# Attention keys of two branches stored tile by tile in pairs, with one mask product per score tile

## The chip, the cores and the metric

The kernel runs on one core of one Trainium2 chip. The metric is device time in microseconds (us) of one execution; lower is better. Beside the time of a run there is the span of a profiled execution, from its first to its last recorded instruction.

## What is computed

One layer of a hybrid block on 512 tokens of width 1024, in fp32: a normalised input projection, an mLSTM branch with 4 heads, a sparse attention branch (NSA) with 8 heads in 2 key groups, an output projection, a gated feed-forward net with a short convolution, a gated extra embedding and a last normalisation. Only the attention scores bear on the change. For each head and query the reference forms three softmaxes: over up to 31 compressed keys, over the selected keys and over a window of keys.

```python
s_c = einsum(qblk, Kc) - slope * dist_c
p_c = where(valid_c, softmax(where(valid_c, s_c, NEG)), 0.0)
s_s = where(valid_s, einsum(qblk, Ksel) - slope * dist_s, NEG)
p_s = softmax(s_s)
s_w = einsum(qblk, kwin) - slope * dist_w
p_w = softmax(where(valid_w, s_w, NEG))
out = gate_c * (p_c @ Vc) + gate_s * (p_s @ Vsel) + gate_w * (p_w @ vwin)
```

With 512 tokens there are 8 selectable blocks and 16 may be selected, so all are; and the window is 512 wide. Both branches are therefore full causal attention over 512 keys, with different keys and values. Below, s is the selected branch, w the window branch, c the compressed one.

## The kernel before, in words

Every fp32 matrix is split into a high and a low part of type float32r and multiplied as three products, so TensorE does several passes for each projection. ScalarE makes the high part (L166), VectorE the low part (L167).

**Order of work.** A `Stream` (L182) holds the projections as jobs that yield matmul by matmul. The attention code is written out by hand, and between its pieces it calls `st.fill(us)`, which emits so many microseconds (by the planner's own costs) of the next projections: filler for TensorE. `FILL2` (L49) is the filler after each of the first four score tiles, `FILL0` and `FILL1` (L47, L48) that of the later ones. When the jobs run out, `fill` emits nothing. `PE_ORDER` is False, so the compiler's list scheduler may still move instructions of an engine past each other, and the order on TensorE is fixed at compile time.

**Keys.** `K` (L464) has 32 columns of compressed keys, then 512 of s, then 512 of w, as high and low part and with rows for position and causal mask of the compressed keys. `key_evac` (L483) writes a branch's columns after its projection: four ScalarE copies (L491) and two VectorE differences (L492) a branch, 512 elements each. The positions come by DMA from `kpos` (L726; made on the host at L1413).

**Scores.** `scores(g, i, r)` (L754) makes one score tile: 128 queries (tile i of 4) of one head (4g + r) against 32 + 2n key columns, n = 128(i + 1). There are 32 such tiles, in the order of `groups` (L861): g = 0 with i = 3, 2, 1, 0, then g = 1 with i = 0, 1, 2, 3. A tile takes these steps:

- products with the high part of the keys (L786) and with the low part (L788), in column regions that each lie in one PSUM bank of 512 columns: one region of 320 columns for i = 0 (two strided pieces of 160), 288 and 256 for i = 1, 416 and 384 for i = 2, and 272, 272 and 512 for i = 3;
- the causal mask of the diagonal 128 columns, added by a bf16 product of an identity with a mask tile (L790): one of 256 columns for i = 0, where s and w are neighbours, and two of 128 columns for the other i;
- row maxima on VectorE: c (L791), s and w together (L793) for i < 3, or s (L795) and w (L796) apart for i = 3;
- three exponentials on ScalarE with row sums (L803), in the order c, s, w;
- the reciprocal (L805), and the scaling of the three parts on GpSimd, for r = 3 partly on VectorE (L810).

**PSUM.** All eight banks belong to one pool: `Sa` (two banks, one buffer), `Sb` (one bank, one buffer), `G`, `T` (two buffers of one bank each) and `V`. Score tiles with i < 3 lie in `Sa`. Those with i = 3 are two tiles, `s_3a` in `Sa` (c and s) and `s_3b` in `Sb` (w), which are released separately. The mLSTM stage uses the same two buffers for `pb` (L999) and `ms` (L1017), the input stage for `pmv` and `pc`.

**Values.** For each group, `value_turn` (L822) transposes four heads' tiles (L835), ScalarE and VectorE split the result (L838, L839), and `value_product` (L842) multiplies it with the values (L843, L845). The scores of the next group are emitted between these units. The last group, g = 1 with i = 3, has no next group; only filler lies between its units.

Of the kernel before, what the change touches and what calls it, by code (L numbers as in the profile page):

```python
# [7 lines left out]
F32 = mybir.dt.float32  # L8
# [3 lines left out]
AF = mybir.ActivationFunctionType  # L12
ALU = mybir.AluOpType
AX = mybir.AxisListType

S = 512
# [29 lines left out]
LOADS = 3  # L46
FILL0 = 0.35  # L47
FILL1 = (2.0, 1.35, 0.9, 0.65)  # L48
FILL2 = 2.5  # L49
MF0 = 1.4  # L50
MF1 = 0.7
MF2 = 1.4
# [16 lines left out]
def f32(ap):  # L69
    return ap.bitcast(F32)  # L70
# [3 lines left out]
def hybrid_block_kernel(ctx: ExitStack, tc: tile.TileContext, a, out):  # L74
    nc = tc.nc
    TE, VE, SE, GE = nc.tensor, nc.vector, nc.scalar, nc.gpsimd
# [5 lines left out]
    tmp = ctx.enter_context(tc.tile_pool(name="tmp", bufs=4))  # L82
    psum = ctx.enter_context(tc.tile_pool(name="psum", bufs=1, space=bass.MemoryType.PSUM))

    def bank(tag, bufs, n, name):
        shape = [128, 512] if n == 1 else [128, n, 512]
        return psum.tile(shape, F32, tag=tag, bufs=bufs, name=name)

    def pSa(name):
        return bank("Sa", 1, 2, name)  # L90

    def pSb(name):
        return bank("Sb", 1, 1, name)

    def pG(name):
        return bank("G", 2, 1, name)

    def pT(name):
        return bank("T", 2, 1, name)
# [6 lines left out]
    def pW(name):  # L106
        wide[0] += 1
        return pG(name) if wide[0] % 2 else pT(name)

    def t2k(name, dt=F32):  # L110
        return tmp.tile([128, 512], dt, tag="t2k", name=name)
# [150 lines left out]
    identb = consts.tile([128, 128], BF, name="identb")  # L262
    maskt = consts.tile([128, 128], BF, name="maskt")
# [199 lines left out]
    NK = 32 + 2 * S  # L463
    K = apool.tile([128, 2, 2, NK], F32R, tag="K", name="K")  # L464
# [18 lines left out]
    def key_evac(br):  # L483
        def evac(ps):
            z = t2k(f"zk{br}")
            VE.tensor_mul(z, ps, rb1)
            sl = slice(32 + br * S, 32 + (br + 1) * S)
            for g in range(2):
                zg = z[g * 64:(g + 1) * 64]
                for half in (g, 1 - g):  # L490
                    SE.activation(K[half * 64:(half + 1) * 64, g, 0, sl], zg, AF.Copy)  # L491
                VE.tensor_sub(K[0:64, g, 1, sl], zg, f32(K[g * 64:(g + 1) * 64, g, 0, sl]))  # L492
        return evac

    cx = {}
# [252 lines left out]
    st.until("mv3")  # L748
    mixa = main.tile([128, 2, 4, S], F32R, tag="mixa", name="mixa")
    mv_done()  # L750

    Ec = {}

    def scores(g, i, r):  # L754
        h = 4 * g + r
        n = (i + 1) * 128
        lq = slice(i * 128, (i + 1) * 128)
        kh, kl = K[:, g, 0], K[0:98, g, 1]
        qa, qb = Q[g][:, 0, r, lq], Q[g][0:98, 1, r, lq]
        nm = tmp.tile([128, 3], F32, tag="nm", name=f"nm{h}_{i}")  # L760
        if i == 0:
            ps = pSa(f"s{h}_{i}")
            v = lambda t: t.rearrange("p (b n) -> p b n", n=512)[:, :, 0:160]
            reg = [(ps[:, 0, 0:320], v(kh[:, 0:1024]), v(kl[:, 0:1024]))]
            cm, sm, wm = ps[:, 0, 0:32], ps[:, 0, 32:160], ps[:, 0, 192:320]
            sw = ps[:, 0, 32:352].rearrange("p (b n) -> p b n", b=2)[:, :, 0:128]
        elif i < 3:
            ps = pSa(f"s{h}_{i}")
            reg = [(ps[:, 0, 0:32 + n], kh[:, 0:32 + n], kl[:, 0:32 + n]),
                   (ps[:, 1, 32:32 + n], kh[:, 32 + S:32 + S + n], kl[:, 32 + S:32 + S + n])]  # L770
            cm, sm, wm = ps[:, 0, 0:32], ps[:, 0, 32:32 + n], ps[:, 1, 32:32 + n]
            sw = ps[:, :, 32:32 + n]
        else:
            p1, p2 = pSa(f"s{h}_{i}a"), pSb(f"s{h}_{i}b")
            reg = [(p1[:, 0, 240:512], kh[:, 0:272], kl[:, 0:272]),
                   (p1[:, 1, 0:272], kh[:, 272:544], kl[:, 272:544]),
                   (p2, kh[:, 544:1056], kl[:, 544:1056])]
            p1f = p1.rearrange("p b n -> p (b n)")
            cm, sm, wm = p1f[:, 240:272], p1f[:, 272:784], p2
            sw = None  # L780
        if i == 0:
            masks = [(sw, maskt[:, None, :].to_broadcast([128, 2, 128]))]
        else:
            masks = [(sm[:, n - 128:n], maskt), (wm[:, n - 128:n], maskt)]
        for ro, rk, _ in reg:
            TE.matmul(ro, qa, rk, start=True, stop=False)  # L786
        for b, (ro, _, rk) in enumerate(reg):
            TE.matmul(ro, qb, rk, start=False, stop=(i == 3 and b == 0))  # L788
        for mo_, mm in masks:
            TE.matmul(mo_, identb, mm, start=False, stop=True)  # L790
        VE.tensor_reduce(out=nm[:, 0:1], in_=cm, axis=AX.X, op=ALU.max, negate=True)  # L791
        if sw is not None:
            VE.tensor_reduce(out=nm[:, 1:3], in_=sw, axis=AX.X, op=ALU.max, negate=True)  # L793
        else:
            VE.tensor_reduce(out=nm[:, 1:2], in_=sm, axis=AX.X, op=ALU.max, negate=True)  # L795
            VE.tensor_reduce(out=nm[:, 2:3], in_=wm, axis=AX.X, op=ALU.max, negate=True)  # L796
        E = (ea if (g + i) % 2 else eb)(f"E{h}_{i}")
        rs = tmp.tile([128, 3], F32, tag="rs", name=f"rs{h}_{i}")
        if r == 0:
            Ec[g, i] = tmp.tile([128, 4, 32], F32, tag="Ec", bufs=2, name=f"Ec{g}{i}")  # L800
        parts = [(Ec[g, i][:, r], cm), (E[:, 0:n], sm), (E[:, n:2 * n], wm)]
        for b, (e, p) in enumerate(parts):
            SE.activation(e, p, AF.Exp, bias=nm[:, b:b + 1], accum_out=rs[:, b:b + 1])  # L803
        rr = tmp.tile([128, 3], F32, tag="rr", name=f"rr{h}_{i}")
        VE.reciprocal(rr, rs)  # L805
        for b in (1, 0, 2):
            e = parts[b][0]

            eng = VE if r == 3 and (b < 2 or i == 0) else GE
            eng.tensor_scalar(e, e, rr[:, b:b + 1], sg[:, i, 3 * h + b:3 * h + b + 1], op0=ALU.mult, op1=ALU.mult)  # L810
        return E
# [53 lines left out]
    for r in range(4):  # L865
        Es.append(scores(*groups[0], r))
        st.spend(score_cost[3])
        st.fill(FILL2)
    pend = None
    for x, (g, i) in enumerate(groups):  # L870
        nxt = groups[x + 1] if x + 1 < len(groups) else None
        if nxt and nxt[0] != g:
            st.until("q11")
        units = value_units(g, i)
        nu = len(units)
        pv = None
        Ns = []
        for u in range(nu):
            got = value_turn(g, i, Es, u, units[u])
            st.spend(0.43)  # L880
            if pend:
                pend()
                st.spend(0.43)
            if u == 0:
                pv = pV(f"pv{g}{i}")

            def product(u=u, got=got, g=g, i=i, pv=pv, vs=units[u][1], last=(u == nu - 1)):
                value_product(pv, vs, *got, u == 0, last)
                if last:
                    value_end(g, i, pv)  # L890
            pend = product
            if nxt:
                while len(Ns) * nu < 4 * (u + 1):
                    st.fill(FILL0)
                    Ns.append(scores(*nxt, len(Ns)))
                    st.spend(score_cost[nxt[1]])
            st.fill(FILL1[i])
        Es = Ns
    pend()


    st.until("mq7")
# [422 lines left out]
    for t in range(NT):  # L1325
        ts = slice(t * 128, (t + 1) * 128)
        ps = (pSb, pV, pT, pT)[t](f"pg1{t}")
        cuts = ((0, 512),) if t < NT - 1 else ((0, CUT), (CUT, 512))
        for part, (c0, c1) in enumerate(cuts):
            if part:  # L1330
                ps = pG("pg1last")
            for k in range(KB):
# [20 lines left out]
def _layouts(inp):  # L1353
# [46 lines left out]
    f = np.float32  # L1400
    p, q = np.arange(128)[:, None], np.arange(128)[None, :]
# [8 lines left out]

    n = np.arange(32)
    t = np.arange(S)
    pos = np.concatenate([16 * np.arange(32) + 31, t, t])  # L1413
    arr["kpos"] = np.stack([pos, np.ones_like(pos)]).astype(f)
    arr["keye"] = np.eye(32, dtype=f)
    slope = 2.0 ** -(np.arange(8) + 1.0)
# [26 lines left out]
```

## Time and profile before

| what | value |
|---|---|
| median of 3 runs | 627.18 us (626.36 to 627.27) |
| profiled execution, its own time | 627.01 us |
| span of the profiled execution | 625.2 us |
| mean granted TensorE clock | 0.996 of full speed |
| busy share: TensorE, VectorE, ScalarE, GpSimd | 98%, 67%, 51%, 10% |

The profiled execution's time is 1.8 us above its span, and 0.17 us below the median. The granted clock is full in every slice of the span but the last. TensorE's busy time is that of matmuls whose ends are modelled and which overlap, so two matmuls that follow each other are compared by their starts, not by their durations.

### The profile page before, as it was taken

The page shows a single profiled execution, that of the slowest core. Times are in us where ns is not written, and L with a number is a line of the kernel's source. Part 1 is how long each engine was busy: PE and PEld are TensorE (multiplying, and loading weights), DVE is VectorE, ACT ScalarE, POOL GpSimd, SP SyncE. Part 2 cuts the span into 40 slices and gives each one's busy share as a digit, 9 for nine tenths or more (in the row PEclk, how much of TensorE's full clock was granted, in tenths as well). Part 3 has the DMA queues.
Part 4 walks back from the last instruction along what each step waited for, and adds up shares of the span by engine and source line. Part 5 has one row for each costly group of instructions (what it writes and reads, how often), then busy time and mean ns, then how long its engine had stood idle before and what let it go on. Part 6 is the DMA issues. An engine that isn't in the chain of part 4 may idle for free. (4 is left out here: it accounts for less than half of the span.)

```text
span 625.2 us, 8416 instructions
## 1 busy us (share of the span) xinstructions
PE 613.9 (98%) x3011; PEld 500.0 (80%) x3011; DVE 417.8 (67%) x800; ACT 317.8 (51%) x665; POOL 62.2 (10%) x132
## 2 busy tenths in 40 slices
PE   9999999999999999999999999999999999999994
PEld 7888877777777777888878888888888888888884
DVE  6988857787777878882977565655556434345386
ACT  7456556677667766653745333334334223233254
POOL 0400009332333400000000000000000000000000
PEclk9999999999999999999999999999999999999998
DMA  8812136112221323122233332233333222634703
GB/s 315 297 63 73 34 102 156 48 35 68 68 65 38 110 93 101 35 69 67 95 108 101 102 97 83 91 100 101 102 101 102 94 94 84 166 103 142 195 1 136
DMA packets 23210, 63.04 MB, mean 101 GB/s; under 512 B 2744, under 2 KB 7736, under 8 KB 23100
## 3 DMA queue, kind: packets, MB, share of 16 engines
q1 hardware_dynamic: 21632, 59.93, 29.5%
q0 software_dynamic: 1248, 2.16, 1.5%
q8 instruction: 24, 0.39, 0.3%
q10 hardware_dynamic: 288, 0.41, 0.2%
q14 instruction: 18, 0.15, 0.1%
HBM read 56.72 MB, written 2.10 MB: 94 GB/s over the span
## 5 line engine op out<-in xcount | busy, mean ns | idle before, releaser
L810 POOL TENSOR_SCALAR E<-E,rr,sg 128x512 f32<-128x512 f32 (+3 forms) x54 | 38.0, 704 | 72.0 <-DVE rr L805 57.8
L839 DVE TENSOR_TENSOR pl<-pt,ph 128x512 fp32r<-128x512 f32 x40 | 27.2, 686 | 7.3 <-ACT ph L838 6.9
L1164 DVE TENSOR_TENSOR zv<-pu,n2rb 128x512 f32<-128x512 f32 x16 | 11.0, 690 | 31.1 <-PE pu L453 31.1
L1167 ACT ACTIVATE u<-zv 128x512 fp32r<-128x512 f32 x16 | 10.1, 632 | 42.6 <-DVE zv L1165 42.6
L838 ACT ACTIVATE ph<-pt 128x512 fp32r<-128x512 f32 x40 | 23.7, 599 | 15.4 <-PE pt L835 14.0
L835 PE MATMUL pt<-cols,E 128*128 128x128 f32 x160 | 26.4, 274 | 0.5 <-DVE E L810 0.4
L1154 DVE TENSOR_TENSOR zg<-pu,n2rb 128x512 f32<-128x512 f32 x16 | 11.1, 692 | 22.3 <-PE pu L453 22.3
L1153 POOL MEMSET zg<- 128x2 f32 x16 | 1.5, 100 | 242.2 <-DVE cv L1159 149.7
L835 PEld LDWEIGHTS pt<-cols,E 128*128 128x128 f32 x160 | 19.9, 140 | 6.4 <-DVE E L810 1.1
L1194 DVE TENSOR_TENSOR X<-pd,X 128x512 f32<-128x512 f32 x8 | 5.5, 692 | 29.2 <-PE pd L453 29.2
L1157 ACT ACTIVATE cv<-zg,cols 128x512 f32<-128x512 f32 x16 | 13.1, 817 | 20.8 <-DVE zg L1154 20.8
L1160 ACT ACTIVATE cv<-cv 128x512 f32<-128x512 f32 x16 | 10.1, 632 | 25.8 <-DVE cv L1159 25.8
L803 ACT ACTIVATE E<-s,nm 128x384 f32<-128x384 f32 (+2 forms) x48 | 22.2, 471 | 0.0
L843 PE MATMUL pv<-ph,V 128*128 128x512 f32 x40 | 18.8, 471 | 0.0
L1168 DVE TENSOR_TENSOR u<-zv,u 128x512 fp32r<-128x512 f32 x16 | 11.0, 691 | 9.8 <-ACT u L1167 9.8
L805 DVE RECIPROCAL rr<-rs 128x3 f32<-128x3 f32 x32 | 5.5, 172 | 16.8 <-ACT E L803 16.7
L845 PE MATMUL pv<-pl,V 128*128 128x512 f32 x40 | 16.5, 411 | 0.1
L793 DVE TENSOR_REDUCE nm<-s 128x2 f32<-128x768 f32 (+2 forms) x24 | 16.3, 680 | 0.0
L286 DVE TENSOR_TENSOR acc<-acc,sq 128x512 f32<-128x512 f32 x21 | 14.4, 684 | 0.1
L803 ACT ACTIVATE Ec<-s,nm 128x32 f32<-128x32 f32 x24 | 6.8, 283 | 13.5 <-DVE nm L793 10.5
L1159 DVE SCALAR_TENSOR_TENSOR cv<-zg,cols,cv 128x512 f32<-128x512 f32 x16 | 12.0, 751 | 0.5
L1158 DVE SCALAR_TENSOR_TENSOR cv<-zg,cols,cv 128x512 f32<-128x512 f32 x16 | 11.9, 746 | 0.0
(1219 smaller groups left out, 2023.3 us busy)
## 6 DMA issues: line engine op xcount, KB each, us to landing
X<-in_xg SPq DMA_DIRECT2D x1, 2048.0 KB, 8.7
xo<-xturn SPq DMA_DIRECT2D x32, 64.0 KB, 2.1
wgr<-in_w_pg SPq DMA_DIRECT2D x4, 512.0 KB, 4.0
s1r<-in_w_s SPq DMA_DIRECT2D x3, 676.0 KB, 8.9
xT<-in_xg SPq DMA_DIRECT2D x3, 514.0 KB, 7.9
rawx<-in_w_mv SPq DMA_DIRECT2D x3, 512.0 KB, 6.7
Q<-hlq POOLq DMA_DIRECT2D x12, 128.0 KB, 3.1
out_y<-xo SPq DMA_DIRECT2D x3, 512.0 KB, 2.6
```

What stands on the lines that cost most here:

```text
L286: return VE.tensor_add(acc[:, :n], acc[:, :n], sq[:, :n])
L793: VE.tensor_reduce(out=nm[:, 1:3], in_=sw, axis=AX.X, op=ALU.max, negate=True)
L803: SE.activation(e, p, AF.Exp, bias=nm[:, b:b + 1], accum_out=rs[:, b:b + 1])
L810: eng.tensor_scalar(e, e, rr[:, b:b + 1], sg[:, i, 3 * h + b:3 * h + b + 1], op0=ALU.mult, op1=ALU.mult)
L835: TE.transpose(pt[:, r * 128:(r + 1) * 128], Es[r][:, c0:c0 + 128], ident)
L838: SE.activation(ph, pt, AF.Copy)
L839: VE.tensor_sub(pl, pt, f32(ph))
L843: TE.matmul(pv, vs, ph, start=first, stop=False)
L845: TE.matmul(pv, vs, pl, start=False, stop=last)
L1157: SE.activation(cv, zg[:, 2:S + 2], AF.Identity, scale=cw(2), bias=cols[:, C_CB + f:C_CB + f + 1])
L1158: VE.scalar_tensor_tensor(cv, zg[:, 1:S + 1], cw(1), cv, op0=ALU.mult, op1=ALU.add)
L1159: VE.scalar_tensor_tensor(cv, zg[:, 0:S], cw(0), cv, op0=ALU.mult, op1=ALU.add)
```

## The change

The key columns are stored in pairs of tiles: after the 32 compressed ones come s and w of tokens 0 to 127, then s and w of tokens 128 to 255, and so on. For query tile i the needed columns are then one run of 32 + 2n, and the two diagonal blocks are neighbours. All tiles lie in one PSUM tile of three banks, for which a pool of its own is closed and opened ahead of the scores and behind them. The filler constant `FILL2` goes from 2.5 to 3.0.

```diff
-FILL2 = 2.5
+FILL2 = 3.0
...
+    def part_banks():
+        if three[0]:
+            three[0].close()
+        three[0] = ExitStack()
+        three[1] = three[0].enter_context(tc.tile_pool(name="three", bufs=1, space=bass.MemoryType.PSUM))
...
+    def pS(name):
+        return bank("S", 1, 3, name, three[1])
...
-            sl = slice(32 + br * S, 32 + (br + 1) * S)
+            def keys(rows, g, part):
+                return K[rows, g, part, 32:NK].rearrange("p (t b n) -> p b t n", b=2, n=128)[:, br]
...
                 for half in (g, 1 - g):
-                    SE.activation(K[half * 64:(half + 1) * 64, g, 0, sl], zg, AF.Copy)
-                VE.tensor_sub(K[0:64, g, 1, sl], zg, f32(K[g * 64:(g + 1) * 64, g, 0, sl]))
+                    SE.activation(keys(slice(half * 64, (half + 1) * 64), g, 0), zg, AF.Copy)
+                VE.tensor_sub(keys(slice(0, 64), g, 1), zg, f32(keys(own, g, 0)))
...
     mv_done()
+    part_banks()
...
+        ps = pS(f"s{h}_{i}")
+        c0, c1 = 0, 288
+        reg = []
+        for b in range((i + 3) // 2):
+            p0 = 224 if b == 0 else 0
+            reg.append((ps[:, b, p0:p0 + c1 - c0], kh[:, c0:c1], kl[:, c0:c1]))
+            c0, c1 = c1, min(c1 + 512, 32 + 2 * n)
+        flat = ps.rearrange("p b n -> p (b n)")
+        cm = flat[:, 224:256]
+        sw = flat[:, 256:256 + 2 * n].rearrange("p (t b n) -> p b t n", b=2, n=128)
+        diag = flat[:, 2 * n:2 * n + 256].rearrange("p (b n) -> p b n", b=2)
...
-        for mo_, mm in masks:
-            TE.matmul(mo_, identb, mm, start=False, stop=True)
+        TE.matmul(diag, identb, maskt[:, None, :].to_broadcast([128, 2, 128]), start=False, stop=True)
...
+        VE.tensor_reduce(out=nm[:, 1:3], in_=sw, axis=AX.XY, op=ALU.max, negate=True)
...
-        parts = [(Ec[g, i][:, r], cm), (E[:, 0:n], sm), (E[:, n:2 * n], wm)]
+        parts = [(Ec[g, i][:, r], cm)] + [(E[:, b * n:(b + 1) * n], sw[:, b]) for b in range(2)]
...
     pend()
+    part_banks()
...
-    pos = np.concatenate([16 * np.arange(32) + 31, t, t])
+    pos = np.concatenate([16 * np.arange(32) + 31, np.repeat(t.reshape(4, 1, 128), 2, 1).reshape(-1)])
```

The regions become 288 columns for i = 0, 288 and 256 for i = 1, 288 and 512 for i = 2, and 288, 512 and 256 for i = 3. `Sa` and `Sb` are taken from the pool `three` outside the score stage.

## Rows read from the trace of the kernel before

**Rows 1.** The page, first part: TensorE's busy time, share and instructions.
```profile
PE 613.9 (98%) x3011; PEld 500.0 (80%) x3011; DVE 417.8 (67%) x800; ACT 317.8 (51%) x665; POOL 62.2 (10%) x132
```
**Rows 2.** Busy time by stretch: start:end, length, then each engine (instructions), granted clock, DMA.
```profile
197.00:217.00 20.00, 20.00 (x114) 15.86 (x112) 16.32 (x38) 14.65 (x44) 9.87 (x14) 1.00 0.27 76
217.00:232.00 15.00, 14.73 (x77) 10.85 (x76) 10.97 (x21) 9.07 (x18) 0.67 (x1) 1.00 0.41 146
```
**Rows 3.** Line L790, weight loads of the mask products: count, ns min/median/max, starts, form.
```profile
L790 PEld LDWEIGHTS <-identb x56: 95/98/153, 86.8 to 213.3; 128*128 128x128 bf16 x56
```
**Rows 4.** Timeline of TensorE: start us, us, line, tile; i = 2, two masks together.
```profile
103.52 0.53 PE L788 MATMUL s<-K,Q 98*128 98x416 f32 x2
103.89 0.29 PE L790 MATMUL s<-maskt,identb 128*128 128x128 bf16 x2
103.99 0.48 PE L449 MATMUL pmo<-x1h,mo0h 128*128 128x512 f32 x1
104.30 0.40 PE L450 MATMUL pmo<-x1lb,mo0h 128*128 128x512 f32 x1
```
**Rows 5.** Timeline of TensorE: i = 0, one mask of 256 columns.
```profile
147.42 0.31 PE L788 MATMUL s<-K,Q 98*128 98x320 f32 x1
147.57 0.29 PE L790 MATMUL s<-maskt,identb 128*128 128x256 bf16 x1
147.62 0.48 PE L449 MATMUL pmq<-x1h,mq0h 128*128 128x512 f32 x1
147.94 0.39 PE L450 MATMUL pmq<-x1la,mq0h 128*128 128x512 f32 x1
```
**Rows 6.** Timeline of TensorE: i = 3, the two masks apart.
```profile
91.31 0.41 PE L788 MATMUL s_3a<-K,Q 98*128 98x272 f32 x2
91.57 0.23 PE L790 MATMUL s_3a<-maskt,identb 128*128 128x128 bf16 x1
...
91.97 0.40 PE L788 MATMUL s_3b<-K,Q 98*128 98x512 f32 x1
92.21 0.23 PE L790 MATMUL s_3b<-maskt,identb 128*128 128x128 bf16 x1
92.25 0.48 PE L449 MATMUL pq<-x1h,q11h 128*128 128x512 f32 x1
92.56 0.39 PE L450 MATMUL pq<-x1la,q11h 128*128 128x512 f32 x1
```
**Rows 7.** Timeline of TensorE: i = 1, the regions of 288 and 256 columns (x2 is both).
```profile
176.62 0.41 PE L786 MATMUL s<-K,Q 128*128 128x288 f32 x2
176.87 0.41 PE L788 MATMUL s<-K,Q 98*128 98x288 f32 x2
177.12 0.29 PE L790 MATMUL s<-maskt,identb 128*128 128x128 bf16 x2
```
**Rows 8.** Line L793, the maxima of s and w of i < 3, all forms.
```profile
L793 DVE TENSOR_REDUCE nm<-s x24: 411/680/948, 104.7 to 198.4; 128x2 f32<-128x768 f32 x8, 128x2 f32<-128x512 f32 x8, 128x2 f32<-128x256 f32 x8
```
**Rows 9.** Timeline of all engines, second score tile: maxima and exponentials.
```profile
93.04 0.68 DVE L795 TENSOR_REDUCE nm<-s_3a 128x1 f32<-128x512 f32 x1
...
93.64 0.68 DVE L796 TENSOR_REDUCE nm<-s_3b 128x1 f32<-128x512 f32 x1
...
93.81 0.29 ACT L803 ACTIVATE Ec<-s_3a,nm 128x32 f32<-128x32 f32 x1 [1.32 <-DVE nm L795]
...
94.09 0.68 ACT L803 ACTIVATE E<-s_3a,nm 128x512 f32<-128x512 f32 x1
...
94.76 0.68 ACT L803 ACTIVATE E<-s_3b,nm 128x512 f32<-128x512 f32 x1
```
**Rows 10.** Waits of the weight loads from 85 to 232 us: us in total, times, longest.
```profile
PEld s L786 <- ACT E L803: 2.4, 9, 0.4
...
PEld s_3a L786 <- ACT E L803: 0.3, 1, 0.3
```
**Rows 11.** Filler of tile pmq from 217.2 to 232.7 us; columns: PE, PEld, DVE busy (instructions).
```profile
217.20:232.70 15.50, 8.89 (x29) 5.19 (x29) 0.69 (x1) 1.00 0.39 136
```

More of the change, by code (lines that the diff above doesn't have):

```diff
@@ L83, in hybrid_block_kernel, with bank @@
     psum = ctx.enter_context(tc.tile_pool(name="psum", bufs=1, space=bass.MemoryType.PSUM))
-    def bank(tag, bufs, n, name):
+    three = [None, None]
+    def part_banks():
[3 more added lines that the diff above has]
+        three[1] = three[0].enter_context(tc.tile_pool(name="three", bufs=1, space=bass.MemoryType.PSUM))
+    def bank(tag, bufs, n, name, pool=None):
         shape = [128, 512] if n == 1 else [128, n, 512]
-        return psum.tile(shape, F32, tag=tag, bufs=bufs, name=name)
+        return (pool or psum).tile(shape, F32, tag=tag, bufs=bufs, name=name)
     def pSa(name):
-        return bank("Sa", 1, 2, name)
+        return bank("Sa", 1, 2, name, three[1])
     def pSb(name):
-        return bank("Sb", 1, 1, name)
+        return bank("Sb", 1, 1, name, three[1])
+    def pS(name):
+        return bank("S", 1, 3, name, three[1])
     def pG(name):
@@ L108, in pW @@
         return pG(name) if wide[0] % 2 else pT(name)
+    part_banks()
+    ctx.callback(lambda: three[0].close())
     def t2k(name, dt=F32):
@@ L486, in evac @@
             VE.tensor_mul(z, ps, rb1)
-            sl = slice(32 + br * S, 32 + (br + 1) * S)
+            def keys(rows, g, part):
+                return K[rows, g, part, 32:NK].rearrange("p (t b n) -> p b t n", b=2, n=128)[:, br]
             for g in range(2):
-                zg = z[g * 64:(g + 1) * 64]
+                own = slice(g * 64, (g + 1) * 64)
+                zg = z[own].rearrange("p (t n) -> p t n", n=128)
                 for half in (g, 1 - g):
-                    SE.activation(K[half * 64:(half + 1) * 64, g, 0, sl], zg, AF.Copy)
-                VE.tensor_sub(K[0:64, g, 1, sl], zg, f32(K[g * 64:(g + 1) * 64, g, 0, sl]))
+                    SE.activation(keys(slice(half * 64, (half + 1) * 64), g, 0), zg, AF.Copy)
+                VE.tensor_sub(keys(slice(0, 64), g, 1), zg, f32(keys(own, g, 0)))
         return evac
@@ L760, in scores @@
         nm = tmp.tile([128, 3], F32, tag="nm", name=f"nm{h}_{i}")
[L761 to L784, printed above, removed]
+        ps = pS(f"s{h}_{i}")
[9 more added lines that the diff above has]
+        diag = flat[:, 2 * n:2 * n + 256].rearrange("p (b n) -> p b n", b=2)
         for ro, rk, _ in reg:
@@ L787, in scores @@
         for b, (ro, _, rk) in enumerate(reg):
-            TE.matmul(ro, qb, rk, start=False, stop=(i == 3 and b == 0))
-        for mo_, mm in masks:
-            TE.matmul(mo_, identb, mm, start=False, stop=True)
+            TE.matmul(ro, qb, rk, start=False, stop=b < len(reg) - 1)
+        TE.matmul(diag, identb, maskt[:, None, :].to_broadcast([128, 2, 128]), start=False, stop=True)
         VE.tensor_reduce(out=nm[:, 0:1], in_=cm, axis=AX.X, op=ALU.max, negate=True)
[L792 to L796, printed above, removed]
+        VE.tensor_reduce(out=nm[:, 1:3], in_=sw, axis=AX.XY, op=ALU.max, negate=True)
         E = (ea if (g + i) % 2 else eb)(f"E{h}_{i}")
@@ L800, in scores @@
             Ec[g, i] = tmp.tile([128, 4, 32], F32, tag="Ec", bufs=2, name=f"Ec{g}{i}")
-        parts = [(Ec[g, i][:, r], cm), (E[:, 0:n], sm), (E[:, n:2 * n], wm)]
+        parts = [(Ec[g, i][:, r], cm)] + [(E[:, b * n:(b + 1) * n], sw[:, b]) for b in range(2)]
         for b, (e, p) in enumerate(parts):
-            SE.activation(e, p, AF.Exp, bias=nm[:, b:b + 1], accum_out=rs[:, b:b + 1])
+            o = e.rearrange("p (t n) -> p t n", n=128) if b else e
+            SE.activation(o, p, AF.Exp, bias=nm[:, b:b + 1], accum_out=rs[:, b:b + 1])
         rr = tmp.tile([128, 3], F32, tag="rr", name=f"rr{h}_{i}")
@@ L899, in hybrid_block_kernel @@
     pend()
+    part_banks()
     st.until("mq7")
```

## The prediction

> **What bounds the kernel now.** I read the page's shares first: TensorE is busy for 613.9 of 625.2 us and nothing else comes near [rows 1]. Busy time of overlapping matmuls can hide a wait, so I went on to the stretches of the stage that changes: from 197 to 217 us TensorE is busy throughout, from 217 to 232 us for 14.73 of 15 us, at full clock [rows 2]. Here TensorE's own work sets the time: what leaves it is gained, unless something new makes it wait. So I read starts of matmuls in the timeline for the price of what leaves, and the waits of the weight loads for what the score tiles cost already. They wait 9 times for an exponential to free a two-bank tile, 2.4 us in all, and once, 0.3 us, for `s_3a` [rows 10].
>
> A difference of 0.2% (1.25 us) is about what a measurement of this kernel tells from none.
>
> **Part 1, the masks.** L790 has 56 weight loads [rows 3]: 8 tiles with one mask, 24 with two. The change leaves 32. The price is the distance from the first mask to the second matmul behind it, since the first one behind still pays for its late weights. Two masks together: 103.89 to 104.30, 0.41 us [rows 4]. One mask of 256 columns: 147.57 to 147.94, 0.37 us [rows 5]; the same distance is 0.36 at two other places of the timeline, and I take 0.36. So a pair that stood together saves 0.05 us. For i = 3 the two masks often stand apart, and each then costs alone: 92.21 to 92.56, 0.35 us, less the 0.24 that a 512-column matmul takes anyway (91.97 to 92.21), is 0.11 [rows 6]. Going through the timeline I count 18 pairs together and 6 apart (five of the eight tiles with i = 3, one with i = 1): 18 x 0.05 + 6 x 0.11 = 1.6 us. The bounds are 24 x 0.05 = 1.2 and 24 x 0.11 = 2.6.
>
> A rule of the Trainium skill speaks against this term. "TensorE: Matmul & The Clock Gate", section "Back-to-back issue gap", gives a matmul of N columns a distance of N / 2.4 + 2.5 ns at full clock, so two of 128 and one of 256 would differ by 2.5 ns, 24 of them by 0.06 us. The rows show twenty times that for a pair. What the time would be if only columns counted is a rival below.
>
> **Part 2, the columns.** For i = 0 a region shrinks from 320 to 288 columns. A product of 320 takes 147.42 to 147.57, 0.15 us [rows 5]; 288 and 256 together take 176.62 to 176.87, 0.25 us, so about 0.13 for 288 [rows 7]. There are 16 such products: 16 x 0.02 = 0.3 us. The other tiles keep their columns in other portions. For i = 2, 416 and 384 take 0.37 us (103.52 to 103.89 [rows 4]); 288 and 512 should take 0.13 and 0.24 (91.97 to 92.21 for 512 [rows 6]), the same. For i = 3, two of 272 take 0.26 (91.31 to 91.57 [rows 6]), and 288 and 256 take 0.25. I take nothing for either; the bounds are 0.01 us for each of the 32 products of i = 2 and 3, 0.3 us to either side.
>
> Saved on TensorE: 1.6 + 0.3 = 1.9 us.
>
> **Part 3, the tile of three banks.** For i = 3, `s_3a` comes free when c and s are exponentiated, while `s_3b` is still used. With one tile everything waits for the third exponential. Two delays come of it:
>
> - VectorE's maxima of s end at 93.72, ScalarE starts at 93.81, and the maxima of w run beside it from 93.64 to 94.32 [rows 9]. One reduction of 1024 elements takes, by the 0.948 us of 768 and the 0.411 of 256 [rows 8], 0.948 + 256 x 0.00105 = 1.22 us. ScalarE starts 1.22 - 0.68 = 0.54 us later.
> - The tile is free at the end of the w exponential instead of the s one, 94.76 to 94.09: 0.67 us later [rows 9].
>
> So the next tile's first product can start up to 1.2 us later, eight times. The first delay rests on ScalarE staying off a tile that VectorE reads; the row shows no more than that it starts 0.09 us after the maxima of its own banks. By the Trainium skill, "PSUM — Partial Sum Buffer", section "PSUM bank collisions raise a hardware error", two engines on one bank and quadrant collide, reads included, so the program must keep them apart; the row agrees, and without that rule the delay would be 0.67 instead of 1.2 us.
>
> What this costs TensorE is not 8 x 1.2 us, because the scheduler puts filler ahead of a blocked score tile. The nearest row is that of the 24 two-bank tiles, which already live with one buffer: 2.4 us [rows 10], 0.1 us a tile. Eight more at that price are 0.8 us, less the 0.3 that `s_3a` waits now: 0.5 us given back. Bounds: below, a gain of 2.7 us if the new order has none of these waits; above, 4.1 us, the third rival.
>
> **Part 4, what goes at no cost.** VectorE has one reduction of 1.22 us instead of two of 0.68 eight times, 1.1 us less, beside TensorE; in this stage it is busy 16.32 of 20 us [rows 2], so that is room and no gain. The key copies and exponentials read or write runs of 128 instead of one run, with as many elements; on VectorE that costs nothing, since 256 columns in runs of 128 (i = 0) lie on one line with 512 and 768 in longer runs: 0.411, 0.680, 0.948 us [rows 8]. No row shows it on ScalarE. The bounds are nothing and, far off, a whole short instruction for each added run, 0.29 us by the 32 columns of c [rows 9]; I take nothing, as on VectorE, which reads the same memory in the same pattern. Of i = 3 it would be six runs more in a tile, 1.7 us; ScalarE, busy 14.65 of 20 us in the last score stage [rows 2], would hide less than that, and the rest would lengthen the chain of part 3 towards the third rival. The pool that closes and opens waits for tiles whose readers are done before the next tile could start anyway: `s_3a` waits for the copies out of `pmv` already, and at the end the first mLSTM product comes after the last value product. `FILL2` moves 4 x 0.5 = 2.0 us of filler ahead, eight matmuls at 0.24 us. It adds no work; no DMA is added, and the queues of SP and POOL keep their order but for weight loads of that filler, which come 2 us earlier.
>
> **Sum.** 1.9 - 0.5 = 1.4 us less. The profiled execution is then 623.8 us in span and 625.6 by its own time of 627.01; against the median of 627.18, 0.17 above it, that is **625.8 us**.
>
> **Rivals.**
>
> 1. *The masks cost by their columns alone.* Then part 1 gives 0.1 us, part 2 0.3, part 3 takes 0.5: 627.3 us. Against it are the 0.41 and 0.36 us of rows 4 and 5; for it, that it rests on a difference of 0.05 us read from few places.
> 2. *The waits take it back.* Each of the eight tiles with i = 3 waits 2.4 / 9 = 0.27 us, the mean of those that wait now [rows 10]: 2.2 us, less the 0.3 of now, against 1.9 saved: 627.2 us. For it: the order on TensorE is fixed ahead, so filler is late or early by what ScalarE is. Against it: 15 of the 24 two-bank tiles wait for nothing.
> 3. *The filler runs out, slower than before.* The place is the last group, g = 1 with i = 3. Its four tiles start one behind the other; three starts at 1.2 us later and 0.54 for the last maxima make the last values late by 3 x 1.2 + 0.54 = 4.1 us. Behind 217.2 us there are 29 filler matmuls of `pmq` [rows 11], 7.0 us at 0.24, now spread between the last units; 2.0 us of it go to the front with `FILL2`, and 4.1 would be spent on waiting. Then nothing is left to cover the last units' splits, and if the scheduler finds none from the mLSTM stage instead, TensorE idles for 4.1 us: 627.2 + 4.1 - 1.9 = 629.4 us. It decides from the point where the delay exceeds the filler left, 7.0 - 2.0 = 5.0 us; with 4.1 this is close. Against it: the units and the filler planned between these tiles may cover part of the delay.
>
> **How the numbers follow.** The forecast has a chance of 0.55, of which 0.47 lie beyond 1.25 us of gain and 0.08 short of it. The first rival has 0.08, the second 0.18, both within 0.2%; the third 0.19, slower. That makes 0.47 faster, 0.34 the same, 0.19 slower. The low end is the upper bound of the masks and of part 2 with no wait added, 2.6 + 0.3 + 0.3 = 3.2 us: 624.0. The high end goes three quarters of the way from no change to the third rival: 628.8. The forecast's own range is 624.0 to 626.9.
>
> **What would show it.** In the profile of the changed kernel L790's successor has 32 weight loads; the distance from a mask to the second matmul behind it is 0.36 us everywhere; the reduction of i = 3 takes 1.22 us, and the c exponential starts behind it. The waits of weight loads for an exponential tell the second rival: 2.9 us for all score tiles would be my sum, 4.6 the rival's. The third shows as idle TensorE, or waits for the value splits, in the last 15 us ahead of the mLSTM stage. The prediction is wrong if the masks' distance is the same as now, or if TensorE has over 2 us more of waits in the score stage.

## The result, and the profile after

The change made the kernel slower: 632.89 us median of 4 runs (631.74 to 633.02) against 627.22 us before in the same job (626.36 to 627.43), a ratio of 1.0089 with the 95% interval [1.0077, 1.0101]. The profiled execution took 632.78 us, its span 631.0 us against 625.2. 5.8 us came into the span, and 1.4 us less had been forecast.

The first part of the page of the changed kernel answers to [rows 1]. TensorE has 24 matmuls less and is busy 1.3 us longer.

```profile
PE 615.2 (98%) x2987; PEld 500.4 (79%) x2987; DVE 417.2 (66%) x792; ACT 319.2 (51%) x665; POOL 62.3 (10%) x132
```

So the loss is not more work (in the 1.3 us are matmuls that a lower clock stretches, see below), and the next view is that of stretches (columns as in [rows 2]).

```profile
197.00:217.00 20.00, 19.87 (x106) 15.33 (x105) 14.12 (x30) 14.58 (x42) 6.33 (x11) 1.00 0.14 47
217.00:232.00 15.00, 14.63 (x74) 11.09 (x74) 12.05 (x23) 11.41 (x27) 3.77 (x4) 1.00 0.61 210
232.00:300.00 68.00, 64.83 (x328) 51.37 (x328) 47.63 (x148) 38.27 (x110) 0.00 (x0) 0.97 0.18 55
```

From 197 to 232 us little is lost beside [rows 2]. Ahead of that, from 150 to 197 us, TensorE idles for 1.68 us, against 0.26 before (first the kernel before, then the changed one). 1.09 us of it is one transpose that waits for GpSimd's scaling of an earlier tile:

```profile
150.00:197.00 47.00, 46.74 (x241) 36.21 (x240) 34.80 (x86) 31.83 (x111) 14.26 (x28) 1.00 0.18 57
```

```profile
150.00:197.00 47.00, 45.32 (x233) 35.75 (x232) 35.10 (x89) 30.53 (x105) 16.39 (x30) 1.00 0.21 60
```

```profile
183.07 0.33 PE L838 MATMUL pt<-cols,E 128*128 128x128 f32 x1 [1.09 <-POOL E L813]
```

Behind 232 us, where the kernel before had finished its attention, TensorE idles for 3.2 us (before: 0.5) and the granted clock is below 1. The same view in steps of 2 us shows where:

```profile
236.00:238.00 2.00, 1.74 (x9) 0.88 (x7) 1.37 (x3) 0.60 (x1) 0.00 (x0) 1.00 0.00 0
238.00:240.00 2.00, 0.38 (x1) 0.06 (x1) 0.91 (x3) 0.67 (x2) 0.00 (x0) 1.00 0.00 0
240.00:242.00 2.00, 1.60 (x6) 1.11 (x7) 1.21 (x3) 1.62 (x5) 0.00 (x0) 0.91 0.00 0
242.00:244.00 2.00, 2.00 (x7) 1.41 (x5) 0.43 (x1) 1.19 (x4) 0.00 (x0) 0.50 0.00 0
244.00:246.00 2.00, 2.00 (x9) 1.45 (x7) 1.20 (x3) 0.00 (x0) 0.00 (x0) 0.73 0.00 0
```

The timeline of TensorE there (start us, us, line, tile, and the idle time ahead with what ended it) names the instructions. The last value product starts at 237.88, where the kernel before has it at 231.89: 6.0 us later. From 226.93 us on the scheduler has put 11 products of the mLSTM stage and the output projection (`pb`, `ms`, `poa`) between the last units; behind them nothing is left to run until ScalarE has written `mixa`.

```profile
237.88 0.50 PE L848 MATMUL pv<-pl,V 128*128 128x512 f32 x1 [0.22 <-DVE pl L842]
240.40 0.73 PE L464 MATMUL poa<-mixa,woa0h 128*128 128x512 f32 x2 [2.01 <-ACT mixa L861]
```

In the kernel before, the last product is followed without a gap by filler of `pmq` and by mLSTM work:

```profile
231.89 0.50 PE L845 MATMUL pv<-pl,V 128*128 128x512 f32 x1
232.22 0.63 PE L453 MATMUL pmq<-x1h,mq7l 128*128 128x512 f32 x2
232.69 0.40 PE L1000 MATMUL pb<-gmr,sel 128*128 128x512 f32 x1
```

From the last value product to the first of `pom`, behind the mLSTM stage, both take 56.2 us, the change in spite of its gap, with those 11 products behind it already: `pom` starts at 288.11 before and 294.05 after, 5.9 us apart, which is the whole difference. The late end of the attention is therefore the thing to explain.

It begins with the score tiles of the last group (g = 1, i = 3). These are the starts of the four c exponentials of the kernel before, and then of the changed one:

```profile
203.22 0.30 ACT L803 ACTIVATE Ec<-s_3a,nm 128x32 f32<-128x32 f32 x1
207.16 0.29 ACT L803 ACTIVATE Ec<-s_3a,nm 128x32 f32<-128x32 f32 x1
210.58 0.28 ACT L803 ACTIVATE Ec<-s_3a,nm 128x32 f32<-128x32 f32 x1
214.48 0.29 ACT L803 ACTIVATE Ec<-s_3a,nm 128x32 f32<-128x32 f32 x1 [2.19 <-DVE nm L795]
```

```profile
206.45 0.29 ACT L806 ACTIVATE Ec<-s,nm 128x32 f32<-128x32 f32 x1 [0.29 <-DVE nm L798]
211.58 0.29 ACT L806 ACTIVATE Ec<-s,nm 128x32 f32<-128x32 f32 x1 [0.80 <-DVE nm L798]
216.09 0.29 ACT L806 ACTIVATE Ec<-s,nm 128x32 f32<-128x32 f32 x1 [0.54 <-DVE nm L798]
220.69 0.29 ACT L806 ACTIVATE Ec<-s,nm 128x32 f32<-128x32 f32 x1 [2.40 <-DVE nm L798]
```

The tiles follow each other every 4.75 us instead of every 3.75 us (a third of the way from first to last), so three steps cost 3.0 us; and the first of them is 3.2 us late already. Together 6.2 us, about the 6.0 by which the last value product is late; the wait at 183.07 us is a part of the 3.2. The filler is gone by then: of the 29 matmuls of [rows 11] 25 are left in the same stretch, the last of them at 226.12 us, and none of them is left for the last 12 us of the attention.

```profile
217.20:232.70 15.50, 6.83 (x25) 4.22 (x24) 1.37 (x2) 1.00 0.60 205
```

The parts that were priced by rows came out. The reduction of i = 3 takes 1.215 us, and the c exponential waits for it:

```profile
L798 DVE TENSOR_REDUCE nm<-s x32: 415/815/1215, 87.4 to 219.4; 128x2 f32<-128x1024 f32 x8, 128x2 f32<-128x768 f32 x8, 128x2 f32<-128x512 f32 x8, 128x2 f32<-128x256 f32 x8
```

There are 32 mask products. From a mask to the second matmul behind it is 0.35 to 0.36 us wherever two of 512 columns follow, as here, against 0.41 in [rows 4]:

```profile
195.40 0.28 PE L796 MATMUL s<-maskt,identb 128*128 128x256 bf16 x1
195.44 0.48 PE L465 MATMUL pmq<-x1la,mq5h 128*128 128x512 f32 x1
195.76 0.39 PE L464 MATMUL pmq<-x1h,mq5h 128*128 128x512 f32 x1
```

Six of the 18 pairs that stood together were ahead of a transpose instead. There the price is smaller: 0.13 us from the first mask to the transpose before (114.71 to 114.84), 0.12 after (116.16 to 116.28).

```profile
114.71 0.29 PE L790 MATMUL s<-maskt,identb 128*128 128x128 bf16 x2
114.84 0.50 PE L835 MATMUL pt<-cols,E 128*128 128x128 f32 x3
```

```profile
116.16 0.28 PE L796 MATMUL s<-maskt,identb 128*128 128x256 bf16 x1
116.28 0.27 PE L838 MATMUL pt<-cols,E 128*128 128x128 f32 x1
```

### The profile page after: what moved, and what is told of

It is laid out like the page before. It is cut to its first block, busy times and chain, and to the rows that moved or that the text cites. A ratio compares the mean times of both kernels' runs of the same rounds, so it can differ in the third digit from the quotient of the medians.

```text
span 631.0 us, 8357 instructions
## 1 busy us (share of the span) xinstructions
PE 615.2 (98%) x2987; PEld 500.4 (79%) x2987; DVE 417.2 (66%) x792; ACT 319.2 (51%) x665; POOL 62.3 (10%) x132
## 5 line engine op out<-in xcount | busy, mean ns | idle before, releaser
L806 ACT ACTIVATE E<-s,nm 128x512 f32<-128x512 f32 (+3 forms) x64 | 32.9, 523 | 0.0
L798 DVE TENSOR_REDUCE nm<-s 128x2 f32<-128x1024 f32 (+3 forms) x32 | 26.1, 814 | 0.0
L806 ACT ACTIVATE Ec<-s,nm 128x32 f32<-128x32 f32 x32 | 9.2, 286 | 17.8 <-DVE nm L798 15.5
L793 PE MATMUL s<-K,Q 128*128 128x288 f32 (+2 forms) x64 | 16.1, 333 | 0.8 <-ACT E L806 0.7
L795 PE MATMUL s<-K,Q 98*128 98x288 f32 (+2 forms) x64 | 15.2, 318 | 0.0
L793 PEld LDWEIGHTS s<-K,Q 128*128 128x128 f32 x64 | 10.5, 188 | 5.1 <-ACT E L806 3.8
```

Source lines behind the costliest of these rows:

```text
L795: TE.matmul(ro, qb, rk, start=False, stop=b < len(reg) - 1)
L798: VE.tensor_reduce(out=nm[:, 1:3], in_=sw, axis=AX.XY, op=ALU.max, negate=True)
L806: SE.activation(o, p, AF.Exp, bias=nm[:, b:b + 1], accum_out=rs[:, b:b + 1])
```

## The experiments

Theory: the tile of three banks makes the tiles of i = 3 follow each other more slowly, `FILL2` spends filler early, and at the end of the attention nothing covers the value splits. Rivals: `FILL2` alone; the stored pairs and their strided access; the clock.

**e1: the change with the old `FILL2`.**

```diff
-FILL2 = 3.0
+FILL2 = 2.5
```

> The changed kernel with FILL2 back at 2.5, nothing else. If the 2.0 us of filler moved to the front are what is missing at the end of the attention, the time falls by about 2 us, to some 631 us. If the tile of three banks makes the last group late whatever is planned, because the scheduler puts filler ahead of a blocked score tile anyway, it stays within 1 us of 632.9. If the filler constant were the whole loss, it would fall to about 626.

Measured: 630.53 us, ratio to the kernel before 1.0054 [1.0039, 1.0069], as expected if the filler moved to the front is missing at the end. 2.4 us of the loss go, 3.6 stay. The first c exponential of the last group starts at 203.58, 0.36 us later than before instead of 3.2; the spacing stays at 4.66 us. So in the changed kernel the late start of the group goes with `FILL2` (and so does the idle time ahead of it: 0.33 us from 150 to 197 us here), and the spacing does not. (It isn't `FILL2`'s in general: in e2, below, with the old value, the group starts 2.4 us late, at 205.59.) A part of what stays is the clock: in the profiled run, the longest of the four with 631.39 us, the granted clock is 0.57 on the mean from 236 to 244 us, 3.4 us of clock missing, a part of it while TensorE idles. The run with the highest mean clock took 629.35 us (more on this in e6).

```profile
236.00:244.00 8.00, 6.58 (x15) 4.87 (x16) 3.95 (x8) 2.93 (x9) 0.00 (x0) 0.57 0.00 0
```

**e2: the tile of three banks alone.** The kernel before, its keys, masks and separate maxima unchanged, but every score tile taken from the one pool of three banks.

```diff
-            ps = pSa(f"s{h}_{i}")
+            ps = pS(f"s{h}_{i}")
...
-            p1, p2 = pSa(f"s{h}_{i}a"), pSb(f"s{h}_{i}b")
+            ps = pS(f"s{h}_{i}")
+            p1, p2 = ps[:, 0:2], ps[:, 2]
```

> The kernel before, with its key order, its two masks, its separate maxima and FILL2 = 2.5, but with every score tile in one tile of three banks. If the one tile is the cause, this is slow by the 5.7 us of the change and the 1.9 us of masks and columns that the change saves: 633 to 635 us, with the last group's tiles some 5 us apart. If the key order or the merged masks are the cause, it stays at 627, within 1 us.

Measured: 631.84 us, 1.008 [1.006, 1.010]: the tile alone costs 4.9 us, less than the 6 to 8 expected. The c exponentials of the last group stand 4.71 us apart. The timeline of all engines around one of them shows the first delay of the prediction's part 3 by itself. The maxima of s and w are separate here, in different banks, and still ScalarE starts behind the maxima of w (L812), which it needs only for its third exponential; in [rows 9] it started 0.09 us behind the maxima of s.

```profile
208.91 0.68 DVE L811 TENSOR_REDUCE nm<-s 128x1 f32<-128x512 f32 x1
209.51 0.68 DVE L812 TENSOR_REDUCE nm<-s 128x1 f32<-128x512 f32 x1
210.28 0.29 ACT L819 ACTIVATE Ec<-s,nm 128x32 f32<-128x32 f32 x1 [1.78 <-DVE nm L812]
...
211.23 0.68 ACT L819 ACTIVATE E<-s,nm 128x512 f32<-128x512 f32 x1
...
212.05 0.75 PE L802 MATMUL s<-K,Q 128*128 128x272 f32 x3
```

The next tile's first product comes at 212.05, behind the last exponential: the second delay. As the row names its releaser, the engines are kept apart by tile in this program, not by bank.

**e3: pairs and one mask for i < 3, two tiles for i = 3.** To keep s apart from w in two tiles, the columns of i = 3 are taken out of the pairs again, in portions of 160 and 384 instead of twice 272, and its masks stay two. `FILL2` is 2.5.

```diff
+            reg = [(p1[:, 0, 352:512], kh[:, 0:160], kl[:, 0:160]),
+                   (three_of(p1[:, 1, 0:384]), own(kh, 0)[:, 1:4], own(kl, 0)[:, 1:4]),
+                   (three_of(p2), own(kh, 1), own(kl, 1))]
```

> The changed kernel with the keys in pairs and one mask for i < 3, but with i = 3 in two tiles of two banks and one, with two masks, as before (s and w are read as strided columns), and FILL2 = 2.5. If the tile of three banks is the cause, the loss is gone and the masks of i = 1 and 2 and the columns of i = 0 remain as gain, 16 x 0.05 + 0.3 = 1.1 us: about 626.1. If the key order is the cause, it stays above 631.

Measured: 628.99 us, 1.003 [1.0019, 1.0041]: still 2.0 us slower than the kernel before, and between the two expectations. The attention ends where it did before (last value product 231.98, first product of `pom` 288.22), so without the tile the delay is gone. What the pairs should have saved isn't there either. In the profiled run, the fastest of the eight with 627.76 us, TensorE idles for 0.5 us at the start of the feed-forward stage, until VectorE has written the low part of a weight (`wu00l`). What the median lies above this run, 1.2 us, no trace shows.

**e4 and e8: the change with the last group's place taken by a short one**, with `FILL2` of 3.0 (e4) and 2.5 (e8). If the delay hurts because it falls at the end, the four tiles of i = 3 at the start of the second half hurt less. The second line keeps neighbouring groups in different buffers for their exponentials.

```diff
-    groups = [(0, i) for i in (3, 2, 1, 0)] + [(1, i) for i in (0, 1, 2, 3)]
+    groups = [(0, i) for i in (3, 2, 1, 0)] + [(1, i) for i in (3, 2, 1, 0)]
...
-        E = (ea if (g + i) % 2 else eb)(f"E{h}_{i}")
+        E = (ea if i % 2 else eb)(f"E{h}_{i}")
```

> The changed kernel with the groups of g = 1 in the order i = 3, 2, 1, 0, so that the four slow tiles of i = 3 fall where much filler is left and the last group is short. If the loss is filler that has run out behind the last group, most of it goes: about 626 to 628 us, with no fall of the clock behind the attention. If the loss is the waits for the tile themselves, wherever they stand, it stays at 631 to 633.

> The changed kernel with the groups of g = 1 in the order 3, 2, 1, 0 and FILL2 = 2.5. If the filler at the front still costs here as it does in the order of the changed kernel (2.4 us), this is 626 to 627. If the filler constant matters only where the long group is last, it stays at the 628.6 of the same order with 3.0.

Measured: 628.60 us, 1.0025 [1.0016, 1.0035], and 628.39 us, 1.0023 [1.0013, 1.0033]. 4.3 us of the loss go with the order alone, and in this order `FILL2` makes no difference that can be told. That is most of the loss, though not all that exhausted filler was expected to explain (626 to 628). The granted clock stays at 1.00 behind the attention.

**e9: the kernel before in the same order**, as the measure for e4 and e8.

> The kernel before (two tiles for i = 3, two masks, FILL2 = 2.5) with the groups of g = 1 in the order 3, 2, 1, 0. If that order is neutral by itself, it stays at 627, and with the changed kernel in the same order at 628.6 the one tile costs more than masks and columns save wherever it stands. If the order is itself worse by 1 to 2 us, to 628 to 629, the change as such is even or a small gain in it.

Measured: 626.12 us, 0.9983 [0.9974, 0.9992]: 1.1 us faster than the kernel before, and the fastest of all that were run. The order is thus worth something by itself, and of e4's gain about 1.1 us is not the tile's doing. Against e9 the change still costs 2.3 to 2.5 us.

**e7: the change with `FILL2` of 1.5**, so that filler moves from the front to the end.

> The changed kernel with FILL2 = 1.5, which leaves 6 us of filler more for later than the changed kernel and 4 us more than with 2.5. If lacking filler at the end of the attention is the loss, the time falls on, towards the 627 minus the 1.9 us that masks and columns save: 627 to 629. If only the tile's spacing counts, it stays at the 630.5 that 2.5 gave.

Measured: 628.25 us, 1.0018 [1.0009, 1.0028], as expected if filler is lacking at the end. With 3.0, 2.5 and 1.5 the loss is 5.7, 3.6 and 1.1 us. The tiles of the last group stand no closer: their c exponentials start from 202.91 to 218.45 us, 5.18 us apart. The weight loads wait longer for exponentials than with the change itself, 5.5 us to 3.8 (waits from 80 to 250 us, first this kernel, then the change):

```profile
PEld s L793 <- ACT E L806: 5.5, 15, 1.0
```

```profile
PEld s L793 <- ACT E L806: 3.8, 11, 0.9
...
PEld poa L464 <- ACT mixa L861: 2.3, 1, 2.3
```

Filler now reaches past the end of the attention, and TensorE is busy from 217 us on:

```profile
217.00:232.00 15.00, 14.97 (x78) 11.51 (x77) 10.00 (x20) 8.81 (x20) 2.40 (x4) 1.00 0.63 211
232.00:300.00 68.00, 67.69 (x347) 54.83 (x346) 48.97 (x150) 40.18 (x114) 0.00 (x0) 1.00 0.20 63
```

So it isn't the sum of the waits on score tiles that decides, but what covers the last units.

**e11: the kernel before with `FILL2` of 3.0.**

> The kernel before with FILL2 = 3.0 alone, nothing else of the change. If the larger FILL2 costs by itself, because it empties the projections' filler before the last group's value units, this kernel is slower by about the 2.4 us that lie between the change (632.9) and the change with 2.5 (630.5): 629.6 us, with the last pmq matmul some 2 us earlier than 232.45 and the last value product later. If it costs only together with the late score tiles (there are 7.0 us of pmq behind 217 us in the kernel before, and 2 us moved ahead still leave 5), it stays within 0.2% of before: 627 to 628 us. I hold the second likelier, 0.65.

Measured: 627.48 us, 1.0009 [1.0001, 1.0018]: 0.6 us. In the change the same edit costs 2.4 us (e1). It needs the late tiles to do that, as expected, though it isn't quite free alone. The last `pmq` matmul starts 3.1 us earlier all the same (229.37) and the last value product 2.1 us later (233.97): a late end of the attention costs little as long as other work covers it, and TensorE idles for 1.4 us from 232 to 300 us here, against 3.2 in the change.

**e6: the clock.** The change, with eight matmuls of 512 columns put behind the last value product, whose result nobody reads.

```diff
+            last_got = got
...
+    keep = pT("keep")
+    for _ in range(8):
+        TE.matmul(keep, Vc[:, 1], last_got[1], start=True, stop=True)
```

> The changed kernel with eight products of 512 columns (1.9 us) into a spare bank in the gap of 2 us behind the last value product, ahead of the first product of the output projection that waits there; the results are not used. If the clock's fall behind that gap is a part of the loss, the granted clock stays at 1.00 and the time falls by up to the 1.7 us that the stretch of 240 to 246 us loses at a clock of 0.91, 0.50 and 0.73: about 631.2. If the clock has no share, the time stays at 632.9 or grows by a few tenths.

Measured: 632.55 us, 1.0089 [1.0074, 1.0104], no different from the change. The granted clock does stay at 1.00 where it fell to 0.50 (this kernel, then the change, from 236 to 248 us):

```profile
236.00:248.00 12.00, 11.58 (x47) 7.86 (x48) 7.99 (x15) 6.91 (x17) 0.00 (x0) 1.00 0.00 0
```

```profile
236.00:248.00 12.00, 9.73 (x35) 6.58 (x34) 6.53 (x13) 5.53 (x13) 0.00 (x0) 0.86 0.00 0
```

and `pom` starts at 293.08 instead of 294.05, 1.0 us earlier. But the feed-forward stage takes it back with a wait of the same size, for a weight's low part that VectorE splits:

```profile
316.53 0.50 PE L458 MATMUL pu<-x2h,wu00l 128*128 128x512 f32 x1 [1.07 <-DVE wu00l L182]
```

So this run shows no gain in the total from a full clock, but it doesn't clear the clock either, since the later wait came with it. The single runs do show a share. Of the change's four runs the one with a mean granted clock of 0.996, that of the kernel before, took 631.74 us, and the three with 0.994 took 632.78 to 633.02. In e1 it is 629.35 us at 0.996 and 630.45 to 631.39 at 0.992 to 0.994; in e2 630.90 and 631.12 at 0.996, 632.56 at 0.994 and 633.71 at 0.992. So in the change a lower mean clock goes with 1.0 to 1.3 us more, and at the clock of the kernel before some 4.5 of its 5.7 us of loss stay. These are few runs.

**e10: e3 in the order of e9**, the candidate to beat both.

> Keys in pairs and one mask for i = 0 to 2 as in the change, two tiles for i = 3 as before, and the second key group in the order 3, 2, 1, 0 (e3 and e9 together). My theory: the three-bank tile and the filler that it exhausts are the whole loss, and the masks' saving is real; with two tiles and the long tiles first nothing is left to take it back but the 160 + 384 columns of i = 3 (0.56 us). Saved on TensorE by masks and columns for i < 3: 16 pairs at 0.05 to 0.06 and 0.3 us = 1.2 us, so 0.6 us below e9 (626.1 in its job): 625.5 us, 0.997 to 0.998 of the kernel before. Rival: the key pairs themselves cost something at the end of the stage or at the feed-forward's start, as e3's 1.8 us above the kernel before leaves open: then this one stays 1.0 us or more above e9, 627.2 to 628 us.

Measured: 629.38 us, 1.0046 [1.0032, 1.006], 3.3 us above e9: the rival's side, and worse than it said. The next two kernels take e10 apart.

**e12: e9 with the portions of 160 and 384**, keys and masks as before.

```diff
-            reg = [(p1[:, 0, 240:512], kh[:, 0:272], kl[:, 0:272]),
-                   (p1[:, 1, 0:272], kh[:, 272:544], kl[:, 272:544]),
+            reg = [(p1[:, 0, 352:512], kh[:, 0:160], kl[:, 0:160]),
+                   (p1[:, 1, 0:384], kh[:, 160:544], kl[:, 160:544]),
```

> e9 (the kernel before, second key group in the order 3, 2, 1, 0) with one thing changed: the first tile of i = 3 is written in portions of 160 and 384 columns instead of 272 and 272, as e10 has to by its pairs. Same columns, same masks. My theory of what e10 lost against e9 (3.3 us): 0.56 us is the portions (16 times 0.035 us, the late weights behind the 160), the rest waits for exponentials that come of another order. Then this kernel stands 0.4 to 0.8 us above e9, 626.5 to 626.9 us. Rival: the portions carry all of it, since each score tile of i = 3 comes late by them and the waits follow: then 628 us or more.

Measured: 628.20 us, 1.0018 [1.0009, 1.0027], 2.1 us above e9: the rival's side, not the 0.4 to 0.8 us of the theory. So 2.1 of the 3.3 us that e10 lost come with the portions alone, without pairs. By the spacing of the matmuls they need 0.56 us more of TensorE (16 times 0.035). In e9's timeline (first fence) the first tile is complete, mask and all, before the second begins; in e12's (second fence) its product of 384 waits its turn behind the second tile's:

```profile
90.15 0.52 PE L786 MATMUL s_3a<-K,Q 128*128 128x272 f32 x2
90.51 0.41 PE L788 MATMUL s_3a<-K,Q 98*128 98x272 f32 x2
90.76 0.23 PE L790 MATMUL s_3a<-maskt,identb 128*128 128x128 bf16 x1
90.82 0.50 PE L786 MATMUL s_3b<-K,Q 128*128 128x512 f32 x1
```

```profile
89.65 0.56 PE L786 MATMUL s_3a<-K,Q 128*128 128x160 f32 x2
90.05 0.24 PE L788 MATMUL s_3a<-K,Q 98*128 98x160 f32 x1
90.16 0.49 PE L786 MATMUL s_3b<-K,Q 128*128 128x512 f32 x1
90.50 0.34 PE L788 MATMUL s_3a<-K,Q 98*128 98x384 f32 x1
90.67 0.39 PE L788 MATMUL s_3b<-K,Q 98*128 98x512 f32 x1
90.90 0.23 PE L790 MATMUL s_3a<-maskt,identb 128*128 128x128 bf16 x1
```

Over the eight tiles the mask of `s_3a` follows its first product after 0.79 us in e9 and 1.28 us in e12 on the mean, so ScalarE gets the first tile half a us later. That this makes up the remaining 1.5 us is a reading, not shown by a run.

**e13: e10 with the mask of i = 1 and 2 split again into two.**

```diff
-            masks = [(diag, maskt[:, None, :].to_broadcast([128, 2, 128]))]
+            masks = [(diag, maskt[:, None, :].to_broadcast([128, 2, 128]))] if i == 0 else [(diag[:, b], maskt) for b in range(2)]
```

> e10 (pairs, two tiles for i = 3, order 3, 2, 1, 0) with the one mask product of 256 columns for i = 1 and 2 split into two of 128 again; nothing else. If the merged mask is worth what the rows say, 0.05 us where a 512-column product stands behind it and 0.01 where a transpose does, these 16 tiles give 0.5 to 0.8 us and this kernel stands that much above e10: 629.9 to 630.2 us. If masks cost by their columns alone, it is equal to e10 (629.4) within 0.2 us. If it is faster than e10, the order of the units and not the mask decides at this size.

Measured: 629.17 us, 1.003 [1.0019, 1.0041], against e10's [1.0032, 1.006]: not to be told apart, and if anything faster; the 629.9 to 630.2 that the rows gave are missed. Summed over the timeline, the time from a mask to the next instruction is 3.1 us here and 2.3 in e10, the 0.8 us that 16 pairs at 0.05 should give. TensorE has that work less and the kernel gets nothing for it.

## Why the prediction was wrong

**What held.** The view of the bound was right as to where TensorE's time goes, but not that what leaves TensorE is gained: in e10 against e13 0.8 us left it and the time did not fall. The prices of instructions were right: 0.36 us behind one mask, 1.22 for the reduction, exponentials in runs of 128 that cost what they did (691 ns at most for 512 columns, against 680 in [rows 9]). Part 1's rival by columns alone has its condition refuted, as the 0.41 of [rows 4] and the 0.36 of after differ by 0.05 us. The prediction took N / 2.4 + 2.5 ns, by which they would differ by 2.5 ns, for a rule of the Trainium skill that speaks against this. It read more into the page than it states: "TensorE: Matmul & The Clock Gate", section "Back-to-back issue gap", gives that formula for an isolated matmul, and says itself that it under-counts small N in a stream of weight loads and matmuls. The 0.05 us of these rows agree with that warning. The 1.6 us of part 1 were somewhat high all the same: I priced all pairs by one that stands ahead of 512-column products, and 6 of the 18 stand ahead of transposes, where the gain is 0.01. That leaves 12 x 0.05 + 6 x 0.01 + 6 x 0.11 = 1.3 us. What parts 1 and 2 give in time can be read from e1 and e2, which differ in them, in the order of the keys and in the reduction: 1.3 us by the medians, with intervals that overlap. Runs of like clock are 1.6 to 2.3 us apart (629.35 against 630.90 and 631.12 at 0.996, 630.62 against 632.56 at 0.994, 631.39 against 633.71 at 0.992), about the 1.9 of the forecast, though they are few.

**The step that failed is the price of part 3**: "the nearest row is that of the 24 two-bank tiles, which already live with one buffer: 2.4 us, 0.1 us a tile", so "0.5 us given back". In place of these 0.5 us the tile alone cost 4.9 (e2). The delay itself was right, up to 1.2 us a tile by the sum and 1.0 measured in the spacing. And the waits for exponentials rose by no more than 1.1 us, from 2.7 to 3.8, between the sum and the 4.6 of the second rival. (The 2.9 named for the sum left out the 0.3 us that `s_3a` waits already; its own terms give 2.4 + 0.8 = 3.2.) But the waits on score tiles are not the price of a late score tile. Filler stands in front of them, and that filler is missing later; the price is paid where it runs out, by instructions that have nothing to do with scores (`mixa` 2.3 us, `pl`). e7 shows it the other way round: more of the named waits, 4.6 us less time. A sign that the prediction had set for its failure did come, if just: TensorE idles for 3.3 us from 85 to 232 us, against 1.2 before, which is over 2 us more.

**Part 4's `FILL2` failed with it.** "It adds no work" is true, and I went from there to no cost. Alone it costs 0.6 us (e11), with the late tiles 2.4 (e1): the two take from the same store of filler.

**The third rival was the right one and mis-sized.** It had the place (the last group), the mechanism (no filler for the last splits) and the sign they show: idle TensorE and waits for value splits ahead of the mLSTM stage. It took 4.1 us for the delay and 629.4 us for the time; measured were 6.2 us and 632.9. The tiles themselves made 3.0 us of this. Missing were the 3.2 us by which the group starts late: the rival began to count at the last group, as if everything ahead of it were on time. Its point of decision, 4.1 us against 5.0 us of filler left, was called close, and its chance of 0.19 was too low for that: a planner that places filler by fixed costs (1.03 for a tile of i = 3, as before) isn't told that the tile takes 1.0 us longer. One condition of the rival was not met, that the scheduler finds no mLSTM work: `pb` runs at 226.93 us, 5.8 us earlier than before. It wasn't enough.

**Part 3's use of the Trainium skill.** "PSUM — Partial Sum Buffer", section "PSUM bank collisions raise a hardware error", speaks of one bank and quadrant. e2's readers are in different banks, which the section lets run side by side, and the row has them one behind the other: the delay of e2 is not asked for by that rule. For the change itself, whose one reduction covers all three banks, no run tells the two reasons apart.

**What stays open.** Why the pairs in two tiles (e10) stand 1.2 us above e12, which has the same portions, though they have less mask work. The wait for `wu00l` (TensorE idles for 0.5 us in e3 and e10, 1.0 in e4, 1.1 in e6) may be a part, but e13 has none and is no faster than e10; what brings it up wasn't tried. Why the change costs 2.3 us over e9 even with the long tiles first (e8), and what the clock's fall alone is worth. The late release and the late start of the exponentials, the two delays of part 3, weren't taken apart either.

## What to carry to other kernels

When filler covers stalls, price a later buffer release by where the filler will be missing, not by the waits that the buffer shows now: add up the delays to the last unit that needs cover, and compare with the filler left there. Two edits that draw on one store of filler are priced together (here 0.6 us alone, 2.4 us with the other), and a planner's cost for a stage is changed with the stage. Here, merging tiles merged their release and kept their readers apart (e2); before a small saving of instructions is taken for that, look at what comes last in the stage, and whether another order puts something shorter there (e9, 1.1 us for one line).

## What the chip showed unexpectedly

- After the thin stretch and the idle 2.01 us from 238 to 240 us the granted clock is 0.91, then 0.50 from 242 to 244 us, which is 1.2 of 2.4 GHz, then 0.73 and 1.00, while TensorE is busy from 240.40 us on. The missing shares of these three rows add up to 0.18 + 1.00 + 0.54 = 1.7 us; with eight unused matmuls in the gap the rows show 1.00. In e2 TensorE was idle for longer, 2.2 of the 4 us from 236 to 240 us, and the clock is 1.00 in the rows behind it: an idle stretch alone doesn't say that the clock falls. The same kernel can go either way: e2's four runs have mean clocks of 0.996 (twice), 0.994 and 0.992.
- Equal columns in unequal portions cost more: 160 and 384 take 0.28 us in e3 (85.20 to 85.48), where twice 272 take 0.25 to 0.26 ([rows 6], and e9's fence above). e3 reads the 384 as strided columns; in e12, where they are not strided, it is 0.29 (86.00 to 86.29).

```profile
85.20 0.45 PE L804 MATMUL s_3a<-K,Q 128*128 128x160 f32 x2
85.48 0.39 PE L804 MATMUL s_3b<-K,Q 128*128 128x512 f32 x1
```
